# Moving the index key's projection behind the query's, and using its spare weight columns for part of the retention value

## The chip, the cores and the metric

The kernel runs on one core of a Trainium2 chip. The metric is device time in microseconds (us), from several executions of the same program on the chip; 0.2% of it is about 1.2 us. The engines are named as in the profile: PE (TensorE, matmuls; PEld is its weight load), DVE (VectorE), ACT (ScalarE), POOL (GpSimd) and SP (SyncE, which here only issues DMAs). Each engine works through its own instructions in the order in which the program gives them.

## What is computed

One decoder layer on a sequence of 512 tokens with 1024 features, in float32. One input projection feeds a retention group (4 heads of 128), a sparse attention group (4 heads of 128) and an indexer (8 heads of 64) that selects 128 keys for each query; then come an output projection, a layer norm and a feed-forward part. The change touches the projections at the start:

```python
proj = x @ w_in
rq, rk, rv, rg, aq, ak, av, iq, ik, iw = jnp.split(proj, IN_SPLITS, axis=-1)
...
rv = rv.reshape(B, S, RET_HEADS, RET_HEAD_DIM)
ret = retention_chunkwise(rq, rk, rv)
...
iq = rope(iq.reshape(B, S, IDX_HEADS, IDX_DIM), positions)
ik = rope(ik[:, :, None, :], positions)[:, :, 0, :]
sel = indexer_topk(iq, ik, iw, topk)
```

`iq` has 512 columns, `ik` 64 and `iw` 8; `rv` has 512. The indexer scores a query against a key as a sum over its heads of `iw` times relu(`iq` . `ik`), and takes the top 128.

## The kernel before

**Number format.** Every matmul factor is split into a high part (a cast to fp32r) and a low part (the remainder). A product is three matmuls: high by high, high by low, low by high (`mm3`, L93 to L96). `split` (L85 to L91) makes the parts: the cast on ACT, the subtraction on the engine that is named, or, when none is named, a negation on ACT followed by an accumulating DMA from POOL.

**Order.** The schedule is written out by hand: instructions run on each engine in program order. Tiles with the same tag share buffers; a tile's new user waits until the old one's readers are done. The tags `wh` and `wl` have four buffers each, PSUM has four buffers of tag `d` (`psd`) and four of tag `u` (`psu`), one bank each.

**First stage, L99 to L211.** The index projection has 640 weight columns in 5 tiles of 128. Tile 0 is the key tile: columns 0 to 31 and 64 to 95 hold the two halves of the index key `ik`, columns 32 to 39 hold `iw`, and the other 56 are zero. Tiles 1 to 4 are the query. The loop at L109 issues the loads for 8 k tiles of 128 features: `xr` (x transposed, 128x512) and `w0r` (the 640 weight columns). The first three `xr` are issued by ACT's queue, everything else by SP's, with the small loads `cols` and `pos_i` before the fourth k tile. The loop at L191 then does, for each k tile: the splits of x and of the weights (for the first k tile the weights' cast is on DVE, x's cast on ACT, the weights' remainder on DVE and x's remainder on POOL; for the others both casts are on ACT and both remainders on DVE), and 15 matmuls (L205): 3 products of 5 tiles, tiles 1 to 4 with 384 tokens (the first 128 need no index query) and tile 0 with all 512. The sums stand in `acc0`, five banks. Nine matmuls on zeros (`warm`, L188) go before.

**The rotary tables** (`rotary_tables`, L124) are made piece by piece between the k tiles: five pieces on DVE, after k tiles 1 to 5, and a last one after k tile 7: Abs and four sines on ACT, then DMAs that spread the tables, two of them issued by ACT (L164). At k tile 5 SP issues the first three loads of 1 MB for the next stage (`fetch`).

**Next stages.** `proj_feature` (L328) makes the four feature projections, 128 weight columns at a time, tile by tile through `weight` and `prepare`. Beside it, a side stream is paced into the main one: `index_rope` (L233) reads `acc0`, rotates key and query, and near its end turns `iw` to token order (L268 to L272: transposes of blocks 1 to 3, then a copy); after it come the logits and the top-k on DVE. `proj_token` (L342) makes `rv` (g = 1), the gate (g = 2) and `av` (g = 0): for each, 4 blocks of 128 tokens, 8 k tiles, 3 products, with 512 weight columns as the moving operand (the line of the matmuls is that of `mm3`). `evac` copies the sums to `tok[g]`. The retention (`ret_keys` to `ret_turn`) reads `tok[1]`, first in `ret_state(0)` (L483). The scores of the indexer stand in `score` (tag `s9`), of which block 0 is not used: the first 128 queries select every key that they may see.

Of the kernel before, what the change touches and what calls it, by code (L numbers as in the profile page):

```python
# [9 lines left out]
F32 = mybir.dt.float32  # L10
F32R = mybir.dt.float32r
I32 = mybir.dt.int32
AF = mybir.ActivationFunctionType
ALU = mybir.AluOpType

P = 128
S = 512
D = 1024
KT = D // P
NB = S // P  # L20
# [3 lines left out]
IH = 8  # L24
# [4 lines left out]
IDX_SCALE = (64.0 ** -0.5) * float(np.float32(8.0 ** -0.5))  # L29
# [24 lines left out]
def hybrid_layer_kernel(ctx: ExitStack, tc: tile.TileContext, xT, x, pos, w0, wf, wt, wo,  # L54
                        wgu, wd, gng, lmg, lmb, lfg, lfb, ident_d, cols_d, masks_d, decay_d, out):
    nc = tc.nc
    V, A, G, T = nc.vector, nc.scalar, nc.gpsimd, nc.tensor
# [3 lines left out]
    wp = ctx.enter_context(tc.tile_pool(name="wp", bufs=3))  # L61
# [5 lines left out]
    def psd(name):  # L67
        return psp.tile([P, 512], F32, tag="d", name=name)

    def psu(name):  # L70
        return psp.tile([P, 512], F32, tag="u", name=name)

    def tmp(name, dt=F32):
        return tp.tile([P, 512], dt, tag="t", name=name)

    def unit(tag, name, dt=F32):
        return big.tile([P, 4, S], dt, tag=tag, name=name)

    def dma(dst, src):
        nc.sync.dma_start(dst, src)  # L80
# [4 lines left out]
    def split(eng_lo, hi, lo, src):  # L85
        A.copy(hi, src)  # L86
        if eng_lo is None:
            A.activation(lo, src, AF.Copy, scale=-1.0)  # L88
            nc.gpsimd.dma_start(lo.bitcast(F32), src, accum_op=ALU.add)  # L89
        else:  # L90
            eng_lo.tensor_tensor(lo, src, hi.bitcast(F32), op=ALU.subtract)  # L91

    def mm3(acc, lh, ll, rh, rl, first, last, **kw):  # L93
        T.matmul(acc, lhsT=lh, rhs=rh, start=first, stop=False, **kw)  # L94
        T.matmul(acc, lhsT=lh, rhs=rl, start=False, stop=False, **kw)  # L95
        T.matmul(acc, lhsT=ll, rhs=rh, start=False, stop=last, **kw)  # L96
# [4 lines left out]
    xh = [xh2[kt // 4][:, kt % 4] for kt in range(KT)]  # L101
    xl = [xl2[kt // 4][:, kt % 4] for kt in range(KT)]
    cols = const.tile([P, 12], F32, name="cols")
    H = S // 2
    pos_i = tp.tile([P, S], I32, tag="t", name="pos_i")[:, :H]
    w0s = [unit(t, f"w0s{i}").rearrange("p k c -> p (k c)") for i, t in enumerate(("s9", "s10", "s0"))]
    w0r = [w0s[kt // 3][:, 640 * (kt % 3):640 * (kt % 3) + 640] for kt in range(KT)]
    xr = [tmp(f"xr{kt}") for kt in range(KT)]
    for kt in range(KT):  # L109
        if kt == 3:  # L110
            dma(cols, cols_d)
            for i in range(2):
                dma(pos_i[64 * i:64 * i + 64],
                    bass.AP(tensor=pos.tensor, offset=pos.offset + H * i, ap=[[0, 64], [1, H]]))
        (nc.scalar.dma_start if kt < 3 else dma)(xr[kt], xT[kt])
        dma(w0r[kt], w0[kt])
    ident = const.tile([P, P], F32, name="ident")
    masks = const.tile([P, 2, P], F32, name="masks")

# [58 lines left out]
    def fetch(n):  # L178
        while len(raws) < min(n, limit[0]):
            raws.append(wp.tile([P, 2, 1024], F32, tag="raw", name=f"raw{len(raws)}"))  # L180
            dma(raws[-1], stream[len(raws) - 1][0])
# [7 lines left out]
    acc0 = [psd("acc0_0")] + [psu(f"acc0_{i}") for i in range(1, 5)]  # L189
    tables_it = rotary_tables()  # L190
    for kt in range(KT):  # L191
        wh = wp.tile([P, 640], F32R, tag="wh", bufs=4, name=f"w0h{kt}")
        wl = wp.tile([P, 640], F32R, tag="wl", bufs=4, name=f"w0l{kt}")
        if kt == 0:
            V.tensor_copy(wh, w0r[kt])
            A.copy(xh[kt], xr[kt])
            V.tensor_tensor(wl, w0r[kt], wh.bitcast(F32), op=ALU.subtract)
            G.tensor_tensor(xl[kt], xr[kt], xh[kt].bitcast(F32), op=ALU.subtract)
        else:
            split(V, xh[kt], xl[kt], xr[kt])  # L200
            split(V, wh, wl, w0r[kt])
        for p, (a, b) in enumerate(((wh, xh), (wl, xh), (wh, xl))):
            for i in (1, 2, 3, 4, 0):
                o = 0 if i == 0 else P
                T.matmul(acc0[i][:, o:], lhsT=a[:, i * P:i * P + P], rhs=b[kt][:, o:],  # L205
                         start=(kt == 0 and p == 0), stop=(kt == KT - 1 and p == 2))

        if kt == 5:
            fetch(3)
        if 1 <= kt <= 5 or kt == KT - 1:  # L210
            next(tables_it)  # L211

    def rope(dst, src, ct, st, lo=0):
        t1 = tmp("rt1")
        t2 = tmp("rt2")
        n = slice(lo, S)
        V.tensor_tensor(t1[:, n], src[:, n], ct[:, n], op=ALU.mult)
        V.tensor_tensor(t2[0:64, n], src[64:128, n], st[64:128, n], op=ALU.mult)
        V.tensor_tensor(t2[64:128, n], src[0:64, n], st[0:64, n], op=ALU.mult)
        if dst is not None:  # L220
            G.tensor_tensor(dst, t1[:, n], t2[:, n], op=ALU.add)
        return t1, t2
# [4 lines left out]
    ql = big.tile([P, 4, M], F32R, tag="s6", name="ql")  # L227
    kk3 = big.tile([P, 3, S], F32R, tag="s8", name="kk3")
    kh, kl = kk3[:, 0], (kk3[:, 1], kk3[:, 2])
    iwr = tmp("iwr")  # L230
    iw = const.tile([P, NB, IH], F32, name="iw")

    def index_rope():  # L233
        G.memset(kk3[:, 1:].bitcast(F32), 0.0)
        A.activation(iwr, acc0[0], AF.Copy, scale=IDX_SCALE)
        t1, t2 = rope(None, acc0[0], CI, SI)
        ks = tmp("ks")
        V.tensor_tensor(ks, t1, t2, op=ALU.add)
        yield 1.7

        def halves_k():
            A.copy(kh, ks)
            for b in (0, 64):
                s, d = slice(b, b + 32), slice(b + 32, b + 64)
                G.tensor_tensor(kl[0][s], ks[s], kh[s].bitcast(F32), op=ALU.subtract)
                nc.gpsimd.dma_start(kl[1][d].bitcast(F32), kl[0][s].bitcast(F32))
                nc.gpsimd.dma_start(kh[d].bitcast(F32), kh[s].bitcast(F32))

        def halves_q(i, qs):
            A.copy(qa[:, i], qs[:, P:])  # L250
            A.copy(qb[:, i], qs[:, P:])
            G.tensor_tensor(ql[:, i], qs[:, P:], qa[:, i].bitcast(F32), op=ALU.subtract)
            if i % 2:
                n = slice(i - 1, i + 1)
                for d, s in ((qa[32:64, n], ql[0:32, n]), (qa[96:128, n], ql[64:96, n]),
                             (qb[0:32, n], ql[32:64, n]), (qb[64:96, n], ql[96:128, n])):
                    nc.gpsimd.dma_start(d.bitcast(F32), s.bitcast(F32))

        rounding = halves_k
        for i in range(4):  # L260
            t1, t2 = rope(None, acc0[1 + i], CI, SI, P)
            qs = tmp("qs")
            V.tensor_tensor(qs[:, P:], t1[:, P:], t2[:, P:], op=ALU.add)
            rounding()
            rounding = lambda i=i, qs=qs: halves_q(i, qs)
            yield 2.3
        rounding()
        yield 3.0  # L268
        iwp = psu("iwp")
        for j in range(1, NB):  # L270
            T.transpose(iwp[:, j * P:(j + 1) * P], iwr[:, j * P:(j + 1) * P], ident)
        A.copy(iw[:, 1:], iwp.rearrange("p (j c) -> p j c", c=P)[:, 1:, 32:32 + IH])  # L272
        yield 3.0

    def prepare():
# [18 lines left out]
    def weight(ahead=3):  # L294
        k = taken[0]
        taken[0] += 1
        while len(ready) < min(k + 1 + ahead, 2 * limit[0]):
            prepare()
        return ready[k]
# [40 lines left out]
    tok = {}  # L340

    def proj_token(g):  # L342
        accs = [(psu if g == 1 and b > 1 else psd)(f"pt{g}_{b}") for b in range(NB)]

        def evac(b):
            if b == 0:
                tok[g] = unit(("s4", "s5", "s6")[g], ("av", "rv", "grg")[g])
            if g == 2:
                sg = tmp("sg")
                A.activation(sg, accs[b], AF.Silu)  # L350
                G.tensor_tensor(tok[g][:, b], sg, gnb, op=ALU.mult)
            else:
                A.copy(tok[g][:, b], accs[b])

        for c in range(4):
            h, l = weight()
            for b in range(NB):
                bs = slice(b * P, b * P + P)
                for k in range(2):
                    kt = 2 * c + k  # L360
                    ks = slice(k * S, k * S + S)
                    mm3(accs[b], xh[kt][:, bs], xl[kt][:, bs], h[:, ks], l[:, ks], kt == 0, kt == KT - 1)
                settle()
                if c == 3:
                    pending.append(lambda b=b: evac(b))
                if b != 1:
                    yield


    score = unit("s9", "score")  # L370

    COST = {1: 0.45, 2: 0.6, 3: 0.75}

# [1064 lines left out]
    for i in range(18):  # L1438
        q, j = WORDER[i]
# [97 lines left out]
    b = NB - 1  # L1537
# [82 lines left out]
```

## Time and profile before

| what | us |
|---|---|
| time, median of 3 runs | 615.69 |
| lowest and highest | 614.97, 615.77 |
| span of the profiled execution | 613.8 |
| PE busy in it | 604.0 |
| DVE busy | 515.8 |
| ACT busy | 350.1 |
| POOL busy | 187.7 |

The span goes from the first to the last instruction of one execution that the profiler recorded; the page gives no other time for that execution. The time of a run is longer by what lies before and after. In a row of the timeline stand the start and the duration in us, the engine, the line of the kernel, the operation, what it writes and reads with the shapes, how many instructions were merged, and in brackets how long the engine was idle before and what ended it. "PEld" and the issue of DMAs ("SPq", "ACTq") have rows of their own. Matmuls are pipelined: the duration of one is longer than the step to the next, so steps are read from the starts.

### The profile page before, as it was taken

How to read it: one execution, taken by the hardware profiler on the slowest of the kernel's cores; microseconds unless marked ns; L12 is line 12 of the kernel's file. 1: busy time of each engine (PE TensorE's matmuls, PEld its weight loads, DVE VectorE, ACT ScalarE, POOL GpSimd, SP SyncE). 2: the span in 40 equal slices, each digit the busy share in tenths (PEclk: the TensorE clock that was granted, in tenths of full speed). 3: DMA queues.
4: the chain of work that ended last, by engine and by line, in shares of the span. 5: the costliest groups of instructions: out<-in, count | busy, mean ns of one | idle time of the engine just before them, and what ended most of it. 6: DMA issues, size and time to landing. Idle time of an engine off the chain costs nothing.

```text
span 613.8 us, 9181 instructions
## 1 busy us (share of the span) xinstructions
PE 604.0 (98%) x3256; PEld 520.1 (85%) x3256; DVE 515.8 (84%) x936; ACT 350.1 (57%) x610; POOL 187.7 (31%) x203
## 2 busy tenths in 40 slices
PE   9999999999999999999999999999999999999994
PEld 7988888888888878889998888888888988887884
DVE  6897687988879877989999899889898788977856
ACT  5643444333242665877756776767777685548300
POOL 1177232421446000342013444435354321214010
PEclk9999999999999999999999999999999999999998
DMA  8877435788443873497247888888878789689502
GB/s 310 287 220 206 147 103 125 177 194 223 128 116 103 288 269 130 111 246 142 86 151 197 165 208 200 176 207 165 206 161 202 163 223 213 150 234 287 196 34 103
DMA packets 43822, 111.30 MB, mean 181 GB/s; under 512 B 4688, under 2 KB 19088, under 8 KB 38144
## 3 DMA queue, kind: packets, MB, share of 16 engines
q1 hardware_dynamic: 20464, 76.23, 36.5%
q0 software_dynamic: 22576, 33.24, 32.2%
q10 hardware_dynamic: 736, 1.25, 0.6%
q8 instruction: 25, 0.41, 0.3%
q14 instruction: 21, 0.17, 0.1%
HBM read 74.52 MB, written 2.10 MB: 125 GB/s over the span
## 4 chain that ended last, share of the span: by engine, by line
PE 88%; DVE 4%; issue 4%; DMA 1%; POOL 1%; ACT 1%; POOLq 0%; DVEq 0%
PE ga L880 10%; PE ga L882 5%; PE gc L880 5%; PE pf L94 5%; PE pf L95 5%; PE pf L96 5%; PE ga L888 5%; PE acc L205 4%; PE gc L882 3%; PE gb L880 3%; PE mx L96 2%; PE mx L94 2%; PE mx L95 2%; PE gc L888 2%; PE pt L94 2%
## 5 line engine op out<-in xcount | busy, mean ns | idle before, releaser
L86 ACT CAST wh<-raw 128x1024 fp32r<-128x1024 f32 x43 | 45.1, 1050 | 51.0 <-issue 20.6
L831 POOL DMA_DIRECT2D t<-t x34 | 29.1, 857 | 87.3 <-DVE t L963 59.0
L94 PE MATMUL pf<-xh,wh 128*128 128x512 f32 x128 | 50.0, 391 | 0.0
L95 PE MATMUL pf<-xl,wh 128*128 128x512 f32 x128 | 50.0, 390 | 0.0
L96 PE MATMUL pf<-xh,wl 128*128 128x512 f32 x128 | 49.9, 389 | 0.0
L831 POOL DMA_DIRECT2D w<-w x34 | 39.7, 1218 | 32.0 <-DVE w L914 23.3
L440 POOL TENSOR_TENSOR rs<-ve,half 128x1 f32<-128x1 f32 (+1 forms) x11 | 11.8, 1069 | 103.7 <-DVE ve L439 103.5
L91 DVE TENSOR_TENSOR wl<-raw,wh 128x1024 fp32r<-128x1024 f32 x24 | 29.1, 1224 | 16.0 <-ACT wh L86 16.0
L94 PE MATMUL pt<-wh,xh 128*128 128x512 f32 x96 | 39.1, 408 | 0.0
L96 PE MATMUL pt<-wh,xl 128*128 128x512 f32 x96 | 37.5, 391 | 0.0
L95 PE MATMUL pt<-wl,xh 128*128 128x512 f32 x96 | 37.4, 390 | 0.0
L89 POOL DMA_DIRECT2D wl<-raw x19 | 16.9, 890 | 59.2 <-ACT wl L88 52.3
L96 PEld LDWEIGHTS pf<-xh,wl 128*128 128x128 f32 x128 | 24.0, 188 | 5.1
L94 PEld LDWEIGHTS pf<-xh,wh 128*128 128x128 f32 x128 | 24.0, 188 | 4.6
L95 PEld LDWEIGHTS pf<-xl,wh 128*128 128x128 f32 x128 | 24.1, 188 | 4.6
L402 DVE MAX8 m<-score 128x8 f32<-128x256 f32 (+2 forms) x48 | 26.8, 558 | 1.1
L403 DVE MATCH_REPLACE8 score<-m,score 128x256 f32<-128x256 f32 (+2 forms) x48 | 26.0, 542 | 0.0
L385 ACT ACTIVATE lg<-lg 128x256 f32<-128x256 f32 (+2 forms) x24 | 10.9, 474 | 24.6 <-PE lg L384 22.6
L89 POOL DMA_DIRECT2D slot<-hu x9 | 10.9, 1336 | 37.6 <-ACT slot L88 37.6
L96 PEld LDWEIGHTS pt<-wh,xl 128*128 128x128 f32 x96 | 18.0, 188 | 3.9
L95 PEld LDWEIGHTS pt<-wl,xh 128*128 128x128 f32 x96 | 18.1, 189 | 3.1
L94 PEld LDWEIGHTS pt<-wh,xh 128*128 128x128 f32 x96 | 18.1, 188 | 3.1
(1175 smaller groups left out, 1979.3 us busy)
## 6 DMA issues: line engine op xcount, KB each, us to landing
graw<-in_wgu_dram SPq DMA_DIRECT2D x22, 1024.0 KB, 5.5
wl<-raw POOLq DMA_DIRECT2D x19, 512.0 KB, 5.8
raw<-in_wf_dram SPq DMA_DIRECT2D x8, 1024.0 KB, 6.7
raw<-in_wo_dram SPq DMA_DIRECT2D x8, 1024.0 KB, 4.9
raw<-in_wt_dram SPq DMA_DIRECT2D x6, 1024.0 KB, 5.3
r<-in_wd_dram SPq DMA_DIRECT2D x12, 512.0 KB, 5.8
w<-w POOLq DMA_DIRECT2D x34, 128.0 KB, 4.2
graw<-graw POOLq DMA_DIRECT2D x17, 256.0 KB, 3.7
```

Source lines behind the costliest of these rows:

```text
L86: A.copy(hi, src)
L89: nc.gpsimd.dma_start(lo.bitcast(F32), src, accum_op=ALU.add)
L91: eng_lo.tensor_tensor(lo, src, hi.bitcast(F32), op=ALU.subtract)
L94: T.matmul(acc, lhsT=lh, rhs=rh, start=first, stop=False, **kw)
L95: T.matmul(acc, lhsT=lh, rhs=rl, start=False, stop=False, **kw)
L96: T.matmul(acc, lhsT=ll, rhs=rh, start=False, stop=last, **kw)
L402: V.max(m8, a)
L403: V.match_replace(out=a, in_to_replace=m8, in_values=a, imm_value=TAKEN)
L831: nc.gpsimd.dma_start(t[:, :Q], t[:, Q:], accum_op=ALU.add)
L880: T.matmul(pair, lhsT=h[:, ws[k]], rhs=parts[q][:, :, k], start=first and k == 0, stop=False, skip_group_check=True)
L882: T.matmul(full[:, :Q], lhsT=l[:, ws[k]], rhs=parts[q][:, 0, k], start=False, stop=k == 3, skip_group_check=True)
L888: T.matmul(gp[n][acc], lhsT=a[:, i * S + k * P:i * S + k * P + P], rhs=parts[q][:, b, k], start=first and j == 0, stop=j == 11, skip_group ...
```

## The change

1. **Loads.** All first loads come from SP's queue, in the order weights, x, weights, x; `w0r` holds only the query's 512 columns. `cols` and `pos_i` go before the third k tile instead of the fourth.
2. **Key tile.** Its weights have a tile of their own (`wkr`, 8 k tiles of 128 columns), loaded behind the others by six DMAs: two with the pieces that hold `ik` and `iw`, four with columns 456 to 511 of `rv`'s weights, into the 56 columns that were zero.
3. **Splits.** For the first k tile the weights are cast on ACT, in two pieces, and x on DVE, and both remainders are on DVE. For the others x's remainder is on POOL.
4. **Matmuls.** The loop does 12 for each k tile, the query's four. Behind the loop the key tile is split at once (1024 columns, cast on ACT, remainder on DVE) and multiplied in 24 matmuls with 512 tokens.
5. **Value.** `index_rope` copies the key's sums unscaled, turns block 0 as well, scales `iw` when it is copied, and copies the 56 value columns of all four blocks to `early_v`, which lies in the unused block of `score`. `proj_token(1)` multiplies 456 columns, and POOL copies the other 56 from `early_v` into `rv`.

```diff
-    w0s = [unit(t, f"w0s{i}").rearrange("p k c -> p (k c)") for i, t in enumerate(("s9", "s10", "s0"))]
-    w0r = [w0s[kt // 3][:, 640 * (kt % 3):640 * (kt % 3) + 640] for kt in range(KT)]
+    w0s = [unit(t, f"w0s{i}") for i, t in enumerate(("s9", "s10"))]
+    w0r = [w0s[kt // 4][:, kt % 4] for kt in range(KT)]
+    wkr = unit("s0", "wkr").rearrange("p k c -> p (k c)")[:, :KT * P]
     xr = [tmp(f"xr{kt}") for kt in range(KT)]
     for kt in range(KT):
-        if kt == 3:
+        if kt == 2:
             dma(cols, cols_d)
...
-        (nc.scalar.dma_start if kt < 3 else dma)(xr[kt], xT[kt])
-        dma(w0r[kt], w0[kt])
+        dma(w0r[kt], w0[kt, :, P:])
+        dma(xr[kt], xT[kt])
+    KV = 456
+    SPARE = ((40, 64), (96, 128))
+    wk3 = wkr.rearrange("p (k c) -> p k c", c=P)
+    for a, z in ((0, 40), (64, 96)):
+        dma(wk3[:, :, a:z], w0.rearrange("k p c -> p k c")[:, :, a:z])
+    for i in range(2):
+        o = KV
+        for a, z in SPARE:
+            dma(wk3[:, 4 * i:4 * i + 4, a:z], wt[1, i, :, :, o:o + z - a])
+            o += z - a
...
-        wh = wp.tile([P, 640], F32R, tag="wh", bufs=4, name=f"w0h{kt}")
-        wl = wp.tile([P, 640], F32R, tag="wl", bufs=4, name=f"w0l{kt}")
+        wh = wp.tile([P, S], F32R, tag="wh", bufs=4, name=f"w0h{kt}")
+        wl = wp.tile([P, S], F32R, tag="wl", bufs=4, name=f"w0l{kt}")
         if kt == 0:
-            V.tensor_copy(wh, w0r[kt])
-            A.copy(xh[kt], xr[kt])
+            for cs in (slice(0, P), slice(P, S)):
+                A.copy(wh[:, cs], w0r[kt][:, cs])
+            V.tensor_copy(xh[kt], xr[kt])
             V.tensor_tensor(wl, w0r[kt], wh.bitcast(F32), op=ALU.subtract)
-            G.tensor_tensor(xl[kt], xr[kt], xh[kt].bitcast(F32), op=ALU.subtract)
+            V.tensor_tensor(xl[kt], xr[kt], xh[kt].bitcast(F32), op=ALU.subtract)
         else:
-            split(V, xh[kt], xl[kt], xr[kt])
+            split(G, xh[kt], xl[kt], xr[kt])
             split(V, wh, wl, w0r[kt])
         for p, (a, b) in enumerate(((wh, xh), (wl, xh), (wh, xl))):
-            for i in (1, 2, 3, 4, 0):
-                o = 0 if i == 0 else P
-                T.matmul(acc0[i][:, o:], lhsT=a[:, i * P:i * P + P], rhs=b[kt][:, o:],
+            for i in range(4):
+                T.matmul(acc0[1 + i][:, P:], lhsT=a[:, i * P:i * P + P], rhs=b[kt][:, P:],
                          start=(kt == 0 and p == 0), stop=(kt == KT - 1 and p == 2))
...
+    wkh = wp.tile([P, KT * P], F32R, tag="wh", bufs=4, name="wkh")
+    wkl = wp.tile([P, KT * P], F32R, tag="wl", bufs=4, name="wkl")
+    split(V, wkh, wkl, wkr)
+    for kt in range(KT):
+        cs = slice(kt * P, kt * P + P)
+        mm3(acc0[0], wkh[:, cs], wkl[:, cs], xh[kt], xl[kt], kt == 0, kt == KT - 1)
...
+    score = unit("s9", "score")
+    early_v = score[:, 0, :NB * (S - KV)].rearrange("p (b c) -> p b c", b=NB)
...
-        A.activation(iwr, acc0[0], AF.Copy, scale=IDX_SCALE)
+        A.copy(iwr, acc0[0])
...
-        for j in range(1, NB):
+        for j in range(NB):
             T.transpose(iwp[:, j * P:(j + 1) * P], iwr[:, j * P:(j + 1) * P], ident)
-        A.copy(iw[:, 1:], iwp.rearrange("p (j c) -> p j c", c=P)[:, 1:, 32:32 + IH])
+        iw3 = iwp.rearrange("p (j c) -> p j c", c=P)
+        A.activation(iw[:, 1:], iw3[:, 1:, 32:32 + IH], AF.Copy, scale=IDX_SCALE)
+        o = 0
+        for a, z in SPARE:
+            A.copy(early_v[:, :, o:o + z - a], iw3[:, :, a:z])
+            o += z - a
...
-        accs = [(psu if g == 1 and b > 1 else psd)(f"pt{g}_{b}") for b in range(NB)]
+        n = KV if g == 1 else S
+        accs = [(psu if g == 1 and b > 1 else psd)(f"pt{g}_{b}")[:, :n] for b in range(NB)]
...
+                if n < S:
+                    G.tensor_copy(tok[g][:, :, n:], early_v)
...
-                A.copy(tok[g][:, b], accs[b])
+                A.copy(tok[g][:, b, :n], accs[b])
...
-                    ks = slice(k * S, k * S + S)
+                    ks = slice(k * S, k * S + n)
...
-    score = unit("s9", "score")
```

## The prediction

> **What bounds the kernel now.** I read the page first, for the shares of the span and the chain that ended last, then the waits of PE, then the timeline of the first 30 us, the only stretch that the change rebuilds.
>
> ```profile
> span 613.8 us, 9181 instructions
> ...
> PE 604.0 (98%) x3256; PEld 520.1 (85%) x3256; DVE 515.8 (84%) x936; ACT 350.1 (57%) x610; POOL 187.7 (31%) x203
> ...
> PE 88%; DVE 4%; issue 4%; DMA 1%; POOL 1%; ACT 1%; POOLq 0%; DVEq 0%
> ```
>
> ```profile
> PE gc L880 <- DVE t L963: 0.6, 1, 0.6
> PE dl L96 <- DMA slot<-hu: 0.2, 1, 0.2
> ```
>
> The second fence is the list of PE's waits (in total, times, longest); beside a wait for the first memset these two are all there is. PE is thus the clock of the whole kernel. A matmul column taken away is worth its time, and a wait put into PE's stream is paid in full. What I look for is whether the change takes out more columns than it puts in waiting.
>
> ```profile
> 5.12 1.54 PE L205 MATMUL acc<-xh,w0h 128*128 128x384 f32 x5
> 6.50 1.10 PE L205 MATMUL acc<-xh,w0l 128*128 128x384 f32 x5
> ...
> 8.37 1.09 PE L205 MATMUL acc<-xh,w0h 128*128 128x384 f32 x5
> ...
> 27.04 1.09 PE L205 MATMUL acc<-xl,w0h 128*128 128x384 f32 x5
> 27.97 0.40 PE L94 MATMUL pf<-xh,wh 128*128 128x512 f32 x1
> ...
> 48.64 0.39 PE L95 MATMUL pf<-xl,wh 128*128 128x512 f32 x1
> ```
>
> This is PE's timeline. Durations overlap, so I take starts. From 27.97 to 48.64 there are 91 steps of 512 columns: 0.227 us each. From 8.37 to 27.04 there are 20 groups of four matmuls of 384 columns and one of 512: 0.9335 us a group, so (0.9335 - 0.227) / 4 = 0.1766 us for 384 columns. A column is worth (0.227 - 0.1766) / 128 = 0.394 ns. The first group takes 6.50 - 5.12 = 1.38 us instead of 0.93: PE is at about half pace until near 5.9.
>
> **The saving.** The value projection of the retention (`proj_token(1)`) has 4 blocks x 8 k tiles x 3 products = 96 matmuls; each loses 56 columns, 22 ns. That is **-2.1 us**. One transpose of 128 columns is added (L270 now starts at block 0), between a quarter of 0.227 and the whole: **+0.1 us**. The key tile's 24 matmuls of 512 columns are only moved behind the query tiles; the number of columns stays. The two small PSUM copies on ACT and the POOL copy into `rv` lie beside PE.
>
> **The first loads.** These rows are the first users of the loads, and DMA's rate in the window from 5 to 10 us (last number, GB/s).
>
> ```profile
> 4.27 0.49 DVE L195 CAST w0h<-w0s 128x640 fp32r<-128x640 f32 x1 [3.13 <-DMA w0s<-in_w_dram]
> 4.44 0.62 ACT L196 CAST xh<-xr 128x512 fp32r<-128x512 f32 x1 [1.01 <-DMA xr<-in_xT_dram]
> ...
> 5.14 1.62 POOL L198 TENSOR_TENSOR xl<-xr,xh 128x512 fp32r<-128x512 f32 x1 [4.69 <-ACT xh L196]
> ...
> 6.08 0.62 ACT L86 CAST xh<-xr 128x512 fp32r<-128x512 f32 x1 [1.02 <-DMA xr<-in_xT_dram]
> ...
> 6.61 0.72 ACT L86 CAST w0h<-w0s 128x640 fp32r<-128x640 f32 x1
> ```
>
> ```profile
> 5.00:10.00 5.00, 5.00 (x25) 4.70 (x25) 3.54 (x8) 2.95 (x6) 1.62 (x1) 1.00 1.01 341
> ```
>
> The first pair of loads shrinks from 576 to 512 KB: 66 kB at 341 GB/s are 0.2 us, so x arrives at 4.25. DVE casts it in about 0.4 (0.49 for 640 columns) where ACT took 0.62, and the first matmul starts at 4.7 instead of 5.12. PE is at half pace there, so 0.4 us are worth 0.2. In the old order the query part without the key would end at 27.97 - 24 x 0.227 = 22.5; now at 22.3. By then the loads are no bound: a k tile takes PE 12 x 0.1766 = 2.1 us, DMA some 1.5 (512 KB at 341), and POOL, which takes the x remainder over from DVE, 1.62. If the one queue started the loads later than two did, up to 0.4 us would be lost here, but the next step shows that this is covered.
>
> **The key tile's own preparation is the new step on the path.** Its cast (`wkh`) stands on ACT behind the last part of the rotary tables, and the remainder `wkl` on DVE behind the cast; PE needs `wkh` for the first key matmul and `wkl` for the third. The tables end on a chain through DVE and ACT:
>
> ```profile
> 8.43 0.29 DVE L136 CAST angles<-pos_i 128x256 f32<-128x256 int32 x1 [0.23 <-DMA pos_i<-in_pos_dram]
> ...
> 9.68 0.69 DVE L91 TENSOR_TENSOR xl<-xr,xh 128x512 fp32r<-128x512 f32 x1
> 10.28 0.82 DVE L91 TENSOR_TENSOR w0l<-w0s,w0h 128x640 fp32r<-128x640 f32 x1
> 11.02 1.34 DVE L130 SCALAR_TENSOR_TENSOR angles<-turns,angles 128x256 f32<-128x256 f32 x3
> 12.27 0.68 DVE L91 TENSOR_TENSOR xl<-xr,xh 128x512 fp32r<-128x512 f32 x1
> ...
> 13.61 0.42 DVE L130 SCALAR_TENSOR_TENSOR angles<-turns,angles 128x256 f32<-128x256 f32 x1
> ...
> 15.06 0.68 DVE L91 TENSOR_TENSOR xl<-xr,xh 128x512 fp32r<-128x512 f32 x1
> ...
> 16.40 1.33 DVE L130 SCALAR_TENSOR_TENSOR angles<-turns,angles 128x256 f32<-128x256 f32 x3
> 17.66 0.68 DVE L91 TENSOR_TENSOR xl<-xr,xh 128x512 fp32r<-128x512 f32 x1
> ...
> 18.99 0.87 DVE L130 SCALAR_TENSOR_TENSOR angles<-turns,angles 128x256 f32<-128x256 f32 x2
> ...
> 20.90 0.69 DVE L91 TENSOR_TENSOR xl<-xr,xh 128x512 fp32r<-128x512 f32 x1
> ```
>
> ```profile
> 21.02 0.42 ACT L156 ACTIVATE angles<-angles 128x256 f32<-128x256 f32 x1 [3.31 <-DVE angles L130]
> ...
> 24.30 1.63 ACTq L164 DMA_DIRECT2D tables<-trig  x2
> 26.04 3.19 ACT L86 CAST wh<-raw 128x1024 fp32r<-128x1024 f32 x3 [1.77 <-PE acc L205]
> ```
>
> ```profile
> 24.29 1.23 DVE L285 TENSOR_TENSOR wl<-raw,wh 128x1024 fp32r<-128x1024 f32 x1
> ```
>
> The five table steps take DVE 1.25 + 1.25 + 1.45 + 1.26 + 1.91 = 7.1 us, start to start. Between them DVE now does one remainder of 512 columns per k tile, 0.60 (9.68 to 10.28). It starts on the second k tile when ACT has cast it: x arrives 131 kB earlier, 6.08 - 0.38 = 5.7; two casts, 0.53 + 0.62; 6.9. So the tables leave DVE at 6.9 + 5 x 0.6 + 7.1 = 17.0, against 20.9 now. From there ACT needs the 26.04 - 21.02 = 5.0 us that it needs now: Abs, a table load, four sines, two DMA issues during which it does nothing else. The issue of those two is 1.63 us of it. `wkh` starts at 17.1 + 5.0 = 22.1, is done at 23.2 (3.19 / 3 a cast), `wkl` at 24.45. PE reaches the key tile at 22.3: it waits 0.9 us for `wkh`, runs two matmuls, waits 0.8 for `wkl`. The other 22 key matmuls, from 24.5 on, end at 24.5 + 22 x 0.227 = 29.5, where the old kernel had its first feature matmul at 27.97: **+1.5 us**, whatever the first matmul gained. Behind the waiting `wkl` on DVE stand the first feature weights (0.69 + 1.23 us), done at 26.4 and due at 29.5; behind `wkh` on ACT the next casts, due later still. The start of DVE on the second k tile may be 6.5 or 7.3 (no earlier load at all): 0.4 either way.
>
> **The key tile's loads.** Six DMAs with pieces of 96 to 160 bytes: 2 x 1024 + 4 x 512 = 4096 pieces for 16 engines, behind the last x. The trace has no such transfer; the nearest are two short windows of the DMA view, from 6.6 to 7.0 us (the 48-byte rows of `cols` among larger ones) and from 29.8 to 30.45 (`ident`, 512-byte rows, then 1 KB).
>
> ```profile
> DMA packets 252, 0.12 MB, mean 289 GB/s; under 512 B 163, under 2 KB 234, under 8 KB 252
> ...
> q1 hardware_dynamic: 220, 0.08, 79.8%
> ```
>
> ```profile
> q1 hardware_dynamic: 189, 0.10, 69.0%
> ```
>
> ```profile
> L80 SPq DMA_DIRECT2D w0s<-in_w_dram x8: 328/420/453, 0.7 to 10.4; - x8
> ...
> DMA to landing us min/median/max: 3.5/4.8/6.1
> ```
>
> The first is 0.798 x 0.4 x 16 / 220 = 23 ns a packet, the second 0.690 x 0.65 x 16 / 189 = 38 ns. The last weights now land by 10.4 + 6.1 = 16.5; with 0.5 MB less in front, by about 15. At 23 ns the pieces end at 15 + 4096 x 23 / 16 = 20.9, at 38 ns at 24.7. Most packets of the first window are under 512 bytes and the larger ones raise its mean, so I take 23 or less: hidden until 22.1, the time at which ACT is free. SP's six issues, at up to 0.8 each as the two on ACT, run to about 15.8 and are hidden too. The first feature weights follow at 20.9 + 3.1 (1 MB at 341) = 24.0, before DVE takes them up at 24.5.
>
> The Trainium skill ("DMA: Bandwidth & Descriptors", Rules for kernel authors and the measured table of Bandwidth) speaks against such pieces: coalesce small transfers, under 512 bytes the engine reads, changes and writes back, and a small transfer costs about 10.5 ns for each packet. If those were paid one after the other, 4096 would be 43 us, and the time some 651. The window from 6.6 us passed 252 packets in 400 ns, 1.6 ns each, so by the trace they are paid on 16 engines side by side.
>
> **The sum.** -2.1 + 0.1 + 1.5 = -0.5 us. The profiled execution has a span of 613.8; the timed runs have a median of 615.69, so 1.9 us lie outside, untouched. **615.2 us.**
>
> **Rivals.** *No wait at the key tile* (faster). Tables, cast and remainder are all done when PE gets there. For: DVE sheds seven x remainders. Against: the chain above is DVE and ACT back to back, and it would have to be 1.7 us shorter. Then -0.2 - 2.1 + 0.1 = -2.2: **613.5**. Part of it would give 614.
>
> *The small pieces land late* (slower). One price decides: above (22.1 - 15) x 16 / 4096 = 28 ns a packet the loads end after ACT is free. At 38 ns, 24.7 instead of 22.1: +2.6 on the forecast, **617.8**.
>
> *The saved columns turn into waits.* In the stretch of the value projection DVE is nearly full with the top-k:
>
> ```profile
> 120.00:150.00 30.00, 30.00 (x140) 25.01 (x139) 27.06 (x73) 12.81 (x15) 7.90 (x8) 1.00 0.80 195
> ```
>
> ```profile
> 149.41 0.68 DVE L477 TENSOR_TENSOR rkd<-rkt,cols 128x512 f32<-128x512 f32 x1
> ```
>
> ```profile
> L483 PEld LDWEIGHTS rkv<-rv,rkd x24: 187/192/192, 152.9 to 175.6; 128*128 128x128 f32 x24
> ```
>
> (27.06 of 30 us.) A shorter projection lets PE come sooner to `rkd`. But that is ready at 150.1 and first loaded at 152.9: 2.8 us of slack against 2.1 saved. If it were all lost: +1.6, **617.3**.
>
> **Chances.** A measurement of this kernel tells about 0.2% (1.2 us) from no change. Forecast with its own range of 614.5 to 616.5: 0.55. No or little wait: 0.26. Late pieces: 0.13. Saving lost: 0.06. So faster 0.26, same 0.55, slower 0.19. The range for 8 in 10 takes in the whole of the first rival and the near part of the two slower ones: 613.3 to 617.4.
>
> **What would show it.** In the profile after: first matmul of L205's loop near 4.7; query part ending near 22.3; in PE's waits new rows for the key matmuls, on ACT's cast and on DVE's remainder, 1.7 us together; ACT's Abs near 17.1 and the cast near 22.1; first feature matmul near 29.5; value matmuls 0.205 us apart. I am wrong on the faster side if the cast starts by 20.5, and on the slower side if the cast's wait ends on the DMA of `wkr`.

## The result and the profile after

The changed kernel takes 624.89 us (median; 622.89 to 625.61) against 615.67 for the kernel before on the same chip. The ratio is 1.0144, 95% interval 1.0126 to 1.0161: **1.4% slower, where 615.2 and no change that a measurement can tell were forecast.** The time lies far above the range of 613.3 to 617.4.

The page of the kernel after: the span and the instructions, and the engines' busy time.

```profile
span 622.6 us, 9206 instructions
...
PE 604.8 (97%) x3257; PEld 520.4 (84%) x3257; DVE 517.8 (83%) x931; ACT 350.1 (56%) x614; POOL 196.3 (32%) x210
```

The span is 8.8 us longer and PE is busy 0.8 us longer, although its matmuls got fewer columns. So PE waits, and something made it slower. The list of PE's waits says for what (us in total, times, longest):

```profile
PE acc L216 <- DVE w0l L91: 5.3, 4, 2.6
PE acc L94 <- ACT wkh L86: 2.0, 1, 2.0
...
PE acc L96 <- DVE wkl L91: 0.5, 1, 0.5
```

The forecast had the two waits at the key tile, 1.7 us together; they are there, 2.5 us. The first row it did not have at all: PE waits four times for the remainder of the *query's* weights, work that DVE has done all along. The timeline of the kernel after shows why:

```profile
6.44 1.29 POOL L91 TENSOR_TENSOR xl<-xr,xh 128x512 fp32r<-128x512 f32 x1 [6.00 <-ACT xh L86]
6.92 1.37 DVE L91 TENSOR_TENSOR w0l<-w0s,w0h 128x512 fp32r<-128x512 f32 x1 [1.45 <-ACT w0h L86]
...
9.79 1.44 DVE L91 TENSOR_TENSOR w0l<-w0s,w0h 128x512 fp32r<-128x512 f32 x1 [0.25 <-ACT w0h L86]
...
11.15 3.41 DVE L141 SCALAR_TENSOR_TENSOR angles<-turns,angles 128x256 f32<-128x256 f32 x3
...
13.01 5.81 POOL L91 TENSOR_TENSOR xl<-xr,xh 128x512 fp32r<-128x512 f32 x4 [0.28 <-ACT xh L86]
...
14.49 1.75 DVE L91 TENSOR_TENSOR w0l<-w0s,w0h 128x512 fp32r<-128x512 f32 x1
...
16.16 1.51 DVE L141 SCALAR_TENSOR_TENSOR angles<-turns,angles 128x256 f32<-128x256 f32 x1
...
16.29 0.98 PE L216 MATMUL acc<-xh,w0l 128*128 128x384 f32 x4 [2.65 <-DVE w0l L91]
...
17.70 1.27 DVE L144 TENSOR_SCALAR turns<-angles 128x256 f32<-128x256 f32 x1
...
19.00 0.29 DVE L145 TENSOR_SCALAR turns<-turns 128x256 f32<-128x256 f32 x1
...
19.67 0.68 DVE L91 TENSOR_TENSOR w0l<-w0s,w0h 128x512 fp32r<-128x512 f32 x1
```

Compare the same DVE operation on the same shape at 6.92 and at 19.67: 1.37 us and 0.68. At 6.92 POOL is in the middle of its own subtraction, which ends at 6.44 + 1.29 = 7.73; DVE's ends at 8.29, 0.56 after it. From 13.01 POOL runs four back to back until 18.82; in that stretch DVE's remainder takes 1.75 and a TENSOR_SCALAR 1.27, the kind that takes 0.29 at 19.00, when POOL is done. Three SCALAR_TENSOR_TENSOR take 3.41 at 11.15 and one takes 1.51 at 16.16; in the kernel before three took 1.34 (at 11.02) and one 0.42 (at 13.61). Together the six slow DVE rows are 0.7 + 0.8 + 2.1 + 1.1 + 1.1 + 1.0 = 6.7 us too long. POOL itself takes 1.29 at 6.44 and 5.81 / 4 = 1.45 in the row of four: here it is hardly held up. **DVE stands still until POOL's subtraction ends.**

Later in the same timeline:

```profile
24.16 0.42 ACT L167 ACTIVATE angles<-angles 128x256 f32<-128x256 f32 x1 [5.53 <-DVE angles L141]
...
29.50 1.04 ACT L86 CAST wkh<-wkr 128x1024 fp32r<-128x1024 f32 x1 [2.08 <-DMA tables<-trig]
...
31.86 0.71 PE L96 MATMUL acc<-xh,wkl 128*128 128x512 f32 x1 [0.53 <-DVE wkl L91]
...
32.36 0.63 PE L94 MATMUL acc<-xh,wkh 128*128 128x512 f32 x1
32.79 0.63 PE L95 MATMUL acc<-xl,wkh 128*128 128x512 f32 x1
...
38.33 0.39 PE L96 MATMUL acc<-xh,wkl 128*128 128x512 f32 x1
38.56 0.39 PE L94 MATMUL pf<-xh,wh 128*128 128x512 f32 x1
```

The tables leave DVE at 24.1, the key's cast starts at 29.50, and the first feature matmul stands at 38.56 instead of 27.97: **10.6 us late.** Between 32.36 and 32.79 a step takes 0.43 us; at the end (38.33 to 38.56) it takes 0.23. The windows of the kernel after (stretch, its length, busy time of PE, PEld, DVE, ACT, POOL, granted clock, DMA share, GB/s) show the clock:

```profile
15.00:20.00 5.00, 2.38 (x12) 2.06 (x12) 4.90 (x6) 2.38 (x4) 3.81 (x3) 1.00 1.02 132
...
30.00:35.00 5.00, 3.88 (x10) 2.77 (x11) 4.39 (x5) 2.44 (x3) 0.00 (x0) 0.70 0.80 193
35.00:40.00 5.00, 5.00 (x23) 4.12 (x22) 0.94 (x1) 1.47 (x2) 0.00 (x0) 0.96 0.80 243
```

0.70 and 0.96 are (0.30 + 0.04) x 5 / 0.5 = 3.4 us at half clock, which cost half of that, 1.7 us. That is part of how PE can be busier with less to do. In the first row DVE is full while PE has 2.4 us of work in 5.

The saving is there. The 96 value matmuls in PE's timeline:

```profile
134.72 0.36 PE L94 MATMUL pt<-wh,xh 128*128 128x456 f32 x1
...
154.54 0.36 PE L96 MATMUL pt<-wh,xl 128*128 128x456 f32 x1
```

These are the first and the last of the 96, so (154.54 - 134.72) / 95 = 0.2086 us a step against 0.227: 1.8 us saved. 10.6 - 1.8 = 8.8 is also the growth of the span, but that the two agree so well is luck: at the last transposes of the retention PE is 9.85 us behind (207.95 against 198.10), and it makes up the rest later.

### The profile page after: what moved, and what is told of

It is laid out like the page before. It is cut to its first block, busy times and chain, and to the rows that moved or that the text cites. A ratio compares the mean times of both kernels' runs of the same rounds, so it can differ in the third digit from the quotient of the medians.

```text
span 622.6 us, 9206 instructions
## 1 busy us (share of the span) xinstructions
PE 604.8 (97%) x3257; PEld 520.4 (84%) x3257; DVE 517.8 (83%) x931; ACT 350.1 (56%) x614; POOL 196.3 (32%) x210
## 4 chain that ended last, share of the span: by engine, by line
PE 86%; DVE 6%; issue 3%; DMA 2%; ACT 1%; POOL 1%; SPq 1%; POOLq 0%; DVEq 0%
PE ga L905 10%; PE ga L907 5%; PE gc L905 5%; PE pf L94 5%; PE pf L95 5%; PE pf L96 5%; PE ga L913 5%; PE gc L907 3%; PE gb L905 3%; PE mx L96 2%; PE mx L94 2%; PE mx L95 2%; PE dl L95 2%; PE dl L94 2%; PE dl L96 2%
## 5 line engine op out<-in xcount | busy, mean ns | idle before, releaser
L94 PE MATMUL pt<-wh,xh 128*128 128x512 f32 (+1 forms) x96 | 38.6, 402 | 0.0
L95 PE MATMUL pt<-wl,xh 128*128 128x512 f32 (+1 forms) x96 | 37.0, 386 | 0.0
L96 PE MATMUL pt<-wh,xl 128*128 128x512 f32 (+1 forms) x96 | 36.7, 382 | 0.0
L95 PEld LDWEIGHTS pf<-xl,wh 128*128 128x128 f32 x128 | 24.1, 188 | 4.6
L988 DVE TENSOR_TENSOR t<-t,gc 128x512 f32<-128x512 f32 x17 | 11.7, 686 | 10.4 <-ACT t L987 10.4
```

## The experiments

Theory A: POOL's subtractions hold DVE up; that delays the weights' remainders and the tables, the tables delay the key tile, and PE's pauses bring the half clock. Theory B: the cause is at the key tile itself, its late place or its small loads. The diffs are against the kernel after, unless another is named.

**x_dve: the x remainders back on DVE.**

```diff
-            split(G, xh[kt], xl[kt], xr[kt])
+            split(V, xh[kt], xl[kt], xr[kt])
```

> The changed kernel with one edit undone: x's remainders are on DVE again instead of POOL. Theory A (while a POOL subtraction runs, a DVE instruction that works on SBUF alone stands still): the 512-wide remainders on DVE go back from 1.4 to 1.75 us to 0.68 us, PE's waits for them, 5.3 us in the changed kernel, go down to 2 us or less (DVE now has two remainders for each k tile and is nearly full), Abs comes near 20 us instead of 24.2, the first feature matmul near 33 instead of 38.6, and the time is 618.6 us, or 620.3 if PE's clock is halved again for 3.4 us at the key tile. Theory B (the 4096 small pieces of the key tile's loads slow SBUF or DVE): DVE's long durations stay, and the time stays near 624.9.

620.27 us; ratio to the kernel before 1.0078 (1.0063 to 1.0094): 4.6 us of the 9.2 are gone, 4.1 by the ratios. PE's waits:

```profile
PE acc L94 <- ACT wkh L86: 1.2, 1, 1.2
...
PE acc L216 <- DVE w0l L91: 1.0, 2, 0.7
...
PE acc L96 <- DVE wkl L91: 0.5, 1, 0.5
```

And its timeline:

```profile
7.96 0.68 DVE L91 TENSOR_TENSOR w0l<-w0s,w0h 128x512 fp32r<-128x512 f32 x1
...
20.84 0.42 ACT L167 ACTIVATE angles<-angles 128x256 f32<-128x256 f32 x1 [3.06 <-DVE angles L141]
...
25.96 1.04 ACT L86 CAST wkh<-wkr 128x1024 fp32r<-128x1024 f32 x1 [1.87 <-PE acc L216]
```

With *more* work on DVE the tables leave it 3.3 us earlier, at 20.84, where they left it before the change (21.02), and the granted clock is 1.00 in every window up to 45 us. For that case 618.6 was expected; the time is 1.7 above it. The first feature matmul stands at 33.44, still 5.5 us late. What stays is the key tile's wait, 1.7 us, and smaller ones for the query's weights.

**pool_alone: the kernel before, with only the x remainders on POOL.**

```diff
-            split(V, xh[kt], xl[kt], xr[kt])
+            split(G, xh[kt], xl[kt], xr[kt])
```

> The kernel before with one part of the change alone: x's remainders of k tiles 1 to 7 on POOL. Theory A: DVE's instructions on SBUF alone grow to 1.2 us and more wherever a POOL subtraction of 1.3 us runs; seven of those cost DVE 9 us and save it 7 x 0.6 = 4.2, so that the tables end some 4 us later and PE, which never waited there, waits for DVE by 2 to 5 us: 617.5 to 620.5 us. Theory B: there are no small pieces in this kernel, DVE only gets less work, and the time is 615.7 or a little less.

619.14 us; 1.0062 (1.0047 to 1.0077). That one word costs 3.6 us (615.52 to 619.14) in a kernel with no key tile behind. One new wait, the DVE rows that lead to it, and the window behind it:

```profile
PE acc L205 <- DVE w0l L91: 2.0, 1, 2.0
```

```profile
8.62 1.38 DVE L136 CAST angles<-pos_i 128x256 f32<-128x256 int32 x1
...
10.42 1.34 DVE L133 TENSOR_SCALAR turns<-angles 128x256 f32<-128x256 f32 x1
...
12.00 1.89 DVE L91 TENSOR_TENSOR w0l<-w0s,w0h 128x640 fp32r<-128x640 f32 x1
```

```profile
15.00:20.00 5.00, 5.00 (x20) 4.46 (x19) 4.83 (x8) 1.25 (x3) 2.96 (x3) 0.66 1.03 432
```

The CAST took 0.29 in the kernel before. The tables leave DVE 4.0 us later (Abs at 25.02 instead of 21.02). 2.0 us of waiting and (1 - 0.66) x 5 = 1.7 us of half clock are the loss. Theory A holds in both directions.

**dense_key: the key tile's weights in one load with pieces of 512 bytes; the 56 value columns are left out.**

```diff
-    for a, z in ((0, 40), (64, 96)):
-        dma(wk3[:, :, a:z], w0.rearrange("k p c -> p k c")[:, :, a:z])
...
-            dma(wk3[:, 4 * i:4 * i + 4, a:z], wt[1, i, :, :, o:o + z - a])
-            o += z - a
+    dma(wk3, w0.rearrange("k p c -> p k c")[:, :, :P])
```

> The changed kernel, but the key tile's weights come in one load of 1024 pieces of 512 bytes; the 56 value columns are left out (zeros in their place), so that part of the retention value is missing from the output. Theory A: the same as the changed kernel within 0.5 us, 624.4 to 625.4. Theory B: most of the 9 us are gone, 618 or less.

624.97 us; 1.0162 (1.0145 to 1.0178), as the kernel after. The small pieces aren't the cause. Its profiled execution has the same loss with another split. The granted clock is 1.00 in every window up to 45 us, but the first two groups of four matmuls take 2.5 us (4.79 to 7.29) instead of 1.6, and the first feature matmul stands at 38.22. The waits for `w0l` are as long in total as in the kernel after, one of them longer:

```profile
PE acc L210 <- DVE w0l L91: 5.2, 4, 3.6
```

**warm_fill: ten matmuls on zeros before the key's, to keep PE from pausing there.**

```diff
+    for _ in range(10):
+        T.matmul(acc0[0], lhsT=cold[:, :P], rhs=cold, start=True, stop=True)
```

> The changed kernel with ten more matmuls on zeros, into the key's bank, between the query part and the key part. If PE's half pace from 32.0 to 35.4 us comes from its having stood idle just before, these keep the clock up: the 22 key matmuls behind the wait take 5.0 us instead of 6.7, and the time falls by 1.0 to 1.7, to about 623.5. If the half pace has another cause, the time stays at 624.9 or rises by up to 0.5.

624.45 us; 1.0148 (1.0132 to 1.0163): where 623.5 was expected if the pause there brings the half clock, nothing is gained that can be told. The key matmuls ran at full clock, but the half clock came earlier, behind a wait of 3.6 us for `w0l`:

```profile
20.00:25.00 5.00, 5.00 (x22) 5.00 (x21) 4.76 (x13) 0.62 (x1) 0.00 (x0) 0.66 0.98 400
```

In this trace the half clock stands behind an earlier pause. One execution doesn't show that filling the last pause moved it there: the added matmuls come later than the pause of 3.6 us.

**key_ahead: x_dve, and the key's split ahead of the tables' last piece on ACT.**

```diff
-        if 1 <= kt <= 5 or kt == KT - 1:
+        if 1 <= kt <= 5:
             next(tables_it)
...
     split(V, wkh, wkl, wkr)
+    next(tables_it)
```

> x_dve, with the key tile's split moved ahead of the tables' last piece on ACT (Abs, sines, two DMA issues). If the second wait is the place behind that piece, wkh is cast near 21 us instead of 26.0, wkl done near 24.4, PE (there at 25.8) no longer waits at the key tile (1.23 + 0.53 us in x_dve) and the time is 1.75 lower: 618.5. If PE waits there for something else, such as the landing of the small pieces, the time stays at 620.3.

617.90 us; 1.0032 (1.0020 to 1.0044). It is 0.6 below what was expected. Both key-tile waits are gone; of the stage's waits these are the largest that are left:

```profile
PE acc L216 <- DVE w0l L91: 1.0, 2, 0.8
PE acc L216 <- ACT w0h L86: 0.7, 1, 0.7
```

The place behind the tables was thus worth 2.4 us (2.8 by the ratios) beyond POOL's share.

**spread: weights before x on ACT and DVE, x on DVE, table pieces only after k tiles 1, 3, 5 and 6, the last two behind the key's split.**

```diff
-            split(G, xh[kt], xl[kt], xr[kt])
-            split(V, wh, wl, w0r[kt])
+            A.copy(wh, w0r[kt])
+            A.copy(xh[kt], xr[kt])
+            V.tensor_tensor(wl, w0r[kt], wh.bitcast(F32), op=ALU.subtract)
+            V.tensor_tensor(xl[kt], xr[kt], xh[kt].bitcast(F32), op=ALU.subtract)
...
-        if 1 <= kt <= 5 or kt == KT - 1:
+        if kt in (1, 3, 5, 6):
             next(tables_it)
...
     split(V, wkh, wkl, wkr)
+    for _ in range(2):
+        next(tables_it)
```

> The changed kernel with three edits: x's remainders on DVE; weights before x on ACT and DVE; the tables' pieces spread, after k tiles 1, 3, 5 and 6, and the last DVE piece and the ACT piece behind the key tile's split. By the account of DVE's minutes each remainder then comes before PE needs it, and PE runs from 4.7 us to the value projection without a wait: first feature matmul near 27.8 (27.97 in the kernel before), 1.6 us saved in the value projection: 613.9 us. If the tables, some 3 us later than before, hold up the indexer, PE waits there and the time is 614.5 to 617.

615.44 us; 0.9996 (0.9986 to 1.0007). The stage is nearly mended, but the time is 1.5 us above what was expected. The features still start at 29.5, 1.5 us later than before the change. With the tables out of the way the cast of the key tile does wait for its loads:

```profile
21.95 1.05 ACT L86 CAST wkh<-wkr 128x1024 fp32r<-128x1024 f32 x1 [4.24 <-DMA wkr<-in_wt_dram]
```

**spread_512: spread, with the value projection back at 512 columns.**

```diff
-        n = KV if g == 1 else S
+        n = S
```

> spread, but the value projection multiplies all 512 columns (the 56 early ones are computed and not used). By the steps in the changed kernel's trace (0.209 us for 456 columns against 0.227 for 512) this costs 96 x 0.018 = 1.7 us over spread; by the forecast's figure of 0.205 it costs 2.1. If the projection's end is set by another engine, it costs under 0.5.

615.96 us; 1.0008 (0.9999 to 1.0018): giving the columns back costs 0.5 us where 1.7 was expected, and the intervals of the two overlap. So it seems that the 1.8 us that PE saves by 155 us don't all reach the end, a second question that the first had covered.

**spread_2q: spread, with the first three x loads back on ACT's queue.**

```diff
-        dma(xr[kt], xT[kt])
+        (nc.scalar.dma_start if kt < 3 else dma)(xr[kt], xT[kt])
```

> spread, with the first three loads of x issued by ACT's queue again, as before the change. If the order of the first loads matters little, as PE is still at half pace there, the time is that of spread within 0.3 us. If one queue brings the first pair earlier as the forecast has it, the first matmul comes near 5.1 instead of 4.7 and the time rises by 0.2 to 0.4.

614.71 us; 0.9985 (0.9976 to 0.9995), 0.7 below spread, where no gain was expected; the intervals of the two overlap. The key's cast starts at 20.09 instead of 21.95 and the features at 28.0, as in the kernel before. DMA moves 343 GB/s from 5 to 10 us instead of 263; it is 255 to 285 in the seven traces that load from one queue and 341 to 357 in the six that load from two. Now a row of PE's waits points to where the saving goes:

```profile
PE ri L525 <- DVE rst L499: 0.6, 1, 0.6
```

and its timeline why (the POOL rows first):

```profile
177.23 1.04 POOL L469 TENSOR_TENSOR rs<-ve,half 128x4 f32<-128x4 f32 x1 [6.38 <-DVE ve L468]
178.26 2.53 POOL L382 TENSOR_TENSOR grg<-sg,gnb 128x512 f32<-128x512 f32 x2
180.75 1.03 POOL L517 TENSOR_TENSOR rstate<-rstate,cols 128x512 f32<-128x512 f32 x1
```

```profile
181.81 0.69 DVE L518 TENSOR_TENSOR rstate<-rstate,rkv 128x512 f32<-128x512 f32 x1 [3.29 <-POOL rstate L517]
182.42 0.68 DVE L499 TENSOR_TENSOR rst<-rs,decay 128x512 f32<-128x512 f32 x1
```

DVE idles 3.29 us for a product that POOL does last in its queue, and `rst`, for which PE waits, stands behind it. In the kernel before `rst` starts at 182.73: DVE comes there only 0.3 us earlier, though PE was 1.6 us ahead. The profiled execution is the second slowest of the twelve (615.82) and has one more wait of 0.6 us, for `gc`, so its waits are not those of the median.

**state_early, before_state, pace.** The first two issue that product three entries earlier in the list of steps, behind the score of the same block, in spread_2q and in the kernel before; pace is spread_2q with the top-k's steps put later.

```diff
-        new = rt["state", b + 1] = tmp(f"rstate{b}")
         if b == 0:
+            new = rt["state", b + 1] = tmp(f"rstate{b}")
...
-            G.tensor_tensor(heads(new), heads(rt["state", b]), per_head(8), op=ALU.mult)
+            new = rt["state", b + 1]
             V.tensor_tensor(new, new, kv, op=ALU.add)
+
+    def ret_decay(b):
+        new = rt["state", b + 1] = tmp(f"rstate{b}")
+        G.tensor_tensor(heads(new), heads(rt["state", b]), per_head(8), op=ALU.mult)
...
-((ret_score, 1),)
+((ret_score, 1), (ret_decay, 1))
...
-((ret_score, 2),)
+((ret_score, 2), (ret_decay, 2))
```

```diff
-    run(proj_token(2), pace(side, 1.8), pace(rets, 1.2))
+    run(proj_token(2), pace(side, 1.5), pace(rets, 1.2))
...
-    run(proj_token(0), pace(tail, 1.4), pace(side, 0.55))
+    run(proj_token(0), pace(tail, 1.4), pace(side, 0.8))
```

> spread_2q with POOL's product for the retention state (rstate times its decay, 128x512, 1.03 us each) issued behind the score of the same block, two steps ahead of the addition, so that it no longer stands in POOL's queue behind the norm's power and two gate products. In spread_2q DVE is idle 3.29 us at 181.8 us for that product, the same as before the change, and PE comes out 0.4 us ahead at 198 us where it was 1.6 us ahead at 176 us. Theory A (the saving of the value projection is eaten at this wait, which hangs on POOL's queue and not on PE): the wait at 181.8 us falls below 1 us, DVE is 2 to 3 us earlier there, PE keeps 1.3 to 1.6 us at 198 us, and the time is 613.7. Theory B (the sum of DVE's work up to 200 us is what sets it): the wait turns up at another place, time as spread_2q, 614.7 within 0.3.

> The kernel before with the same product moved in the same way, nothing else. Its PE waits 0.3 us for rst and none of the 1.6 us is there to be kept. Theory A: 615.3 (0.3 of the wait for rst goes). Theory B: as before, 615.5 within 0.2. If it falls by as much as state_early does against spread_2q, the gain is that of the product alone and says nothing about the saving.

> spread_2q with fewer of the top-k's steps beside the third token projection (a share of 1.5 in place of 1.8 a step) and more beside the last (0.8 in place of 0.55): the same work on DVE, put later. Theory B (DVE's sum up to 200 us): PE keeps about 1 us more at 198 us, 613.9. Theory A (POOL's queue): DVE waits longer for the product at 181.8 us, nothing gained, 614.7 within 0.3.

state_early takes **613.84 us; 0.9964 (0.9952 to 0.9975)**: faster than the kernel before by 1.9 us. before_state takes 615.29; 0.9989 (0.9978 to 1.0001): the product alone gives at most what a measurement can just tell. The product is early in both kernels, and all runs of state_early (612.71 to 614.14) lie below all of before_state (614.51 to 616.99): the change with its first stage mended is worth 1.4 us there. Against spread_2q the ratios give state_early 1.3 us, with intervals that just part. pace takes 614.27; 0.9977 (0.9968 to 0.9986), which can't be told from spread_2q's 0.9985. In state_early both waits of DVE for the product, 5.5 us in spread_2q, are gone, and DVE is 6 us earlier at `rst`:

```profile
176.10 0.68 DVE L499 TENSOR_TENSOR rst<-rs,decay 128x512 f32<-128x512 f32 x1
```

What PE keeps is read at the last transposes of the retention. They start at 198.10 in the kernel before, 198.08 in before_state, 197.68 in spread_2q and 196.04 in state_early: PE is ahead by 0.4 us in spread_2q and by 2.1 in state_early, and the product alone gains nothing there. Of the 2.1, 0.4 is an earlier start of the features (27.6; 27.3 in pace, whose first stage is the same as that of spread_2q with 28.0, so this is what one execution differs from the next); the rest, 1.7, is about the whole saving. This is one execution of each kernel, and state_early's is the fastest of its five: by the times, 1.4 us are shown.

Pace reached `rst` at 178.90 with the 3.29 us wait still in place, and its last transposes start at 195.73. So the two theories are not exclusive: DVE's queue ahead of `rst` held both the wait and the top-k, and in the traces either can be taken away. What pace put later came up as a new wait in the attention, 0.7 us (PE's waits in pace):

```profile
PE apt L602 <- DVE ast L593: 0.7, 1, 0.7
```

## Why the prediction was wrong

| step of the prediction | forecast | after |
|---|---|---|
| first matmul | 4.7 | 4.65 |
| tables leave DVE, Abs starts | 17.0, 17.1 | 24.16 |
| from Abs to the key's cast | 5.0 | 5.3 |
| from the cast to the third key matmul | 2.4 | 2.4 |
| the other 22 key matmuls | 5.0 | 6.7 |
| first feature matmul | 29.5 | 38.56 |
| value projection | -2.1 | -1.8 |

**The step that failed** is "the tables leave DVE at 6.9 + 5 x 0.6 + 7.1 = 17.0". It took the five table steps from the kernel before, at durations from a stretch in which POOL was idle (0.00 us busy from 10 to 20), and counted the seven x remainders only as work taken off DVE; on POOL's side it said "POOL, which takes the x remainder over from DVE, 1.62" was covered by PE's 2.1 us a k tile. POOL was covered; DVE was not. A POOL subtraction stops DVE for up to its own 1.3 us, twice the 0.6 us of the operation that it relieved DVE of. So the tables left DVE at 24.16: that is +7.0 of the +9.1 at the first feature matmul, and the six slow DVE rows of the kernel after make up 6.7 of it. x_dve and pool_alone show it from both sides: without POOL the changed kernel's tables are 3.3 us earlier, with POOL the old kernel's are 4.0 later.

The kernel before's own timeline had the sign of it, and I didn't use it (the rows of DVE and POOL):

```profile
34.32 1.29 POOL L245 TENSOR_TENSOR kk<-ks,kk 32x512 fp32r<-32x512 f32 x1 [1.92 <-ACT kk L242]
34.57 0.55 DVE L219 TENSOR_TENSOR rt<-acc,tables 64x384 f32<-64x384 f32 x1
35.15 0.87 DVE L263 TENSOR_TENSOR qs<-rt,rt 128x384 f32<-128x384 f32 x1
...
40.92 0.56 DVE L263 TENSOR_TENSOR qs<-rt,rt 128x384 f32<-128x384 f32 x1
40.95 1.41 POOL L252 TENSOR_TENSOR ql<-qs,qa 128x384 fp32r<-128x384 f32 x1
```

Behind a POOL operation that began first L263, which reads twice from SBUF, takes 0.87 and ends 0.41 after it. At 40.92 it begins 0.03 before one and takes 0.56; there POOL's operation is the slow one, 1.41 against 1.00 to 1.01 in its three other rows. The 1.62 us of POOL at 5.14, which the forecast took for POOL's price, is of this kind too: DVE had begun a remainder at 4.80. L219, which reads one of its inputs from PSUM, is not slowed. The Trainium skill ("SBUF — State Buffer", Who interferes with whom) states this rule: a DVE instruction with two SBUF inputs, and a cast or tensor_scalar in its fast modes, shares a port pair with a GpSimd instruction that reads SBUF, and whichever comes second stands still for the whole of the other. The rows above agree (0.68 against 1.37, CAST 0.29 against 1.38, POOL's 1.00 against 1.41); the prediction should have weighed it as the rule that speaks against the change.

**The half clock** was not in the forecast either: +1.7 us, because the pauses that it follows were not.

**The key tile** was right in kind: its waits came where the forecast put them, with their 2.4 us between cast and third matmul. With x on DVE they are 1.7 us together, the sum in the forecast, though 4 us later. That the sum is the same is luck, as PE came to the key tile late too, at 25.8 instead of 22.3; that DVE would be relieved was the part that never came true.

**The first loads** were right at the first matmul, 4.65, but not behind it. The forecast counted on 341 GB/s; from 5 to 10 us the kernel after moved 276, and the third k tile's x reached ACT at 8.61 instead of 7.65. What this cost the kernel after isn't shown, as PE waited there for DVE and not for x. Between spread and spread_2q, which differ only in the queue of these loads, it is 1.5 us at the first feature matmul.

**The small pieces** were right: hidden, as dense_key shows. In the DMA view of the kernel after from 11 to 22 us (40 slices of 0.275 us) they are the packets under 512 bytes:

```profile
GB/s 395 365 343 350 387 365 380 410 395 402 395 410 417 381 340 289 238 200 173 123 79 81 109 50 127 103 83 112 24 89 319 45 0 238 238 447 357 357 387 387
DMA packets 5170, 2.86 MB, mean 260 GB/s; under 512 B 4298, under 2 KB 4298, under 8 KB 5081
```

The rate falls while they pass, from the 15th slice to the 30th: about 14.9 to 19.3 us, ten before the cast at 29.50. 4.4 us on 16 engines for 4096 are 17 ns a packet, an estimate, where the forecast took 23 or less. Once the tables are out of the way they do set the cast, at 21.95 in spread and 20.09 in spread_2q. The forecast had ACT free at 22.1, so the rival of late pieces was a closer call than its 0.13 says.

**The saving** was mis-sized a little: a step is 0.2086 us and not 0.205, so 456 columns don't lie on the straight line between 384 and 512 that the forecast drew. The rival that it turns into waits, which got 0.06, was right in part and wrong about the place: not `rkd`, which I examined, but a later `rst`, behind POOL's product. I had read the DVE window up to 150 us only, and the wait stands at 182 in the kernel before already, where it cost PE little. So "a matmul column taken away is worth its time" held for the projection itself; how much of it reaches the end hangs on the engines behind it.

## What to carry to other kernels

An engine with idle time is not free room: before work is moved to GpSimd, look at what VectorE does in the same stretch, and find a row of the trace in which the two run at once. Time saved on the bound engine is kept only if the engines that feed it later are early too; follow each wait of theirs, also those that cost nothing yet. When a small reordering gives a large loss, put back the parts one by one in both kernels: here one word held nearly half of it.

## What the runs showed of the hardware

- While a GpSimd TENSOR_TENSOR of 128x512 that began first runs, these VectorE operations stand still until it ends: TENSOR_TENSOR with both inputs in SBUF 0.68 to 1.37 and 1.75, SCALAR_TENSOR_TENSOR 0.42 to 1.51, TENSOR_SCALAR 0.29 to 1.27, CAST 0.29 to 1.38. When VectorE began first, GpSimd was the slow one: 1.41 instead of 1.00 (L252 of the kernel before). Operations with one input in SBUF went on beside it: L219 of the kernel before, and the top-k's MAX8 (0.69 at 177.98 in state_early, inside a GpSimd TENSOR_TENSOR from 177.84 to 179.11).
- With the first x loads on a second queue DMA moved 341 to 357 GB/s from 5 to 10 us, with all on one queue 255 to 285.
- The half clock lasted 3.4 us each time, behind pauses of 2.0 us (pool_alone), 2.0 (after) and 3.6 (warm_fill), while dense_key's pause of 3.6 us brought none, and in the kernel after itself the pause of 2.65 us before 16.29 didn't either (clock 1.00 from 15 to 20). So the length of one pause doesn't decide. The Trainium skill ("TensorE: Matmul & The Clock Gate", Part 1) gives a free-running window of 3413 ns: one that is idle brings the half clock, and one of work ends it. The 3.4 us agree with the second, but pauses shorter than the window were followed by the half clock too. How busy a window may be wasn't tried.
